# A latent-diffusion layer on one core: the second half of the second adaLN slab pair is multiplied as a high and a low part

## The chip, the core and the metric

The kernel runs on one core of one Trainium2 chip. The metric is the device time of one execution in microseconds; the median of three runs of the kernel before is 637.93 us (636.94 to 639.37). The numbers of the profile come from one further execution of the same program, recorded by the hardware profiler.

## The reference, cut to what matters

One layer of a latent-diffusion backbone works on 1024 latent tokens of width 1024, with one conditioning vector `c`, 256 context tokens and one learned vector `c_ctx`.

```python
def adaln(cond, w_ada, b_ada):
    m = jax.nn.silu(cond) @ w_ada + b_ada
    return jnp.split(m, 3, axis=-1)          # shift, scale, gate

shift, scale, gate = adaln(c, w_ada, b_ada)
shift_c, scale_c, gate_c = adaln(c_ctx, w_ada, b_ada)
h  = rmsnorm(x, norm_g) * (1 + scale[:, None]) + shift[:, None]
hc = rmsnorm(ctx, norm_g) * (1 + scale_c) + shift_c
q, k, v, za, u, bg, cg, zc = jnp.split(h @ w_in, SPLIT_POINTS, axis=-1)
...
attn = neighbourhood_attention(...) * silu(za)
conv = bg * conv3(cg * u) * silu(zc)
out  = x + gate[:, None] * (concat([attn, conv]) @ w_out)
```

The change is in the first line of `adaln`: the product of the two silu vectors (for `c` and for `c_ctx`, two columns side by side) with the shift and scale columns of `w_ada`.

## The kernel before, in words

**Number formats.** Nearly all matrix products are made as three products of two-part numbers: an operand is split into a high part, rounded to the reduced fp32 format (`F32R`), and a low part, which is the rest. ScalarE makes the high part (`act.copy`, shown as CAST), VectorE the low part (`dve.tensor_tensor(..., ALU.subtract)`).

**Stages.** In the first stage (up to about 78 us of the profile) the kernel loads x, the adaLN columns of `w_ada` and the first weight columns of `w_in`. It makes the modulation vectors `ab` (shift and scale by feature, for `c` and for `c_ctx`), the normed, transposed and modulated activations `h` (eight tiles `hh[k]`, `hl[k]`, high and low, one for each 128 features), and with each finished `h[k]` three columns of projections (`first_columns`, accumulators `acc`). Then come 32 projection tiles (`pacc`), 32 attention steps with further projections between them (`pu`), and the output projection (`pout`).

**The adaLN slabs.** The 2 x 1024 columns (shift, scale) are taken in four groups m = 0..3 of 256 shift columns (j = 0) and 256 scale columns (j = 1). `load_slab(m, j)` loads 1024 rows of 256 columns as `slabs[m, j]`, 128 partitions by 8 by 256. `products(m, j)` multiplies the slab, eight contraction steps, into one PSUM tile `mods[m]`, columns 0 to 255 for j = 0 and 256 to 511 for j = 1. For m = 0 and 1 this is done in fp32 with `c2`, the two silu columns. For m = 2 and 3 `split(m, j, part)` first makes `highs[j]` and `lows[j]` (names `slabh` and `slabl` in the profile), in two halves of four contraction steps, and `products` multiplies both with `c4`, four columns: the two silu columns in high part and their low part. The result then has four rows. `row_copy(m)` copies these to SBUF, `modulation(m)` transposes them and adds them up into the columns `ab[:, 2m:2m+2]`, with two further additions on VectorE if there are four rows. Group m is needed for `turn(half, 2m)` and `turn(half, 2m+1)`: `turn` writes the modulated high part with ScalarE (`h<-tr,ab`), the fp32 value with ScalarE or VectorE (`hw<-tr,ab`), and the low part with VectorE (`h<-hw,h`). `half` is 0 for the first 512 tokens and 1 for the other 512.

**Order.** In the first stage all engines and the SyncE queue run strictly in the order in which the code is written (`strict[:] = every + [sp]`): each instruction is chained behind the one before it on its engine. Loads come from SyncE in the order slabs (0,0) and (0,1), x tiles 0 to 3, weight chunk 0, x 4 and 5, chunk 1, x 6 and 7, slabs (1,0) and (1,1), chunks 2 and 3, slab (2,0). Slabs (1,·), (2,·) and (3,·) share three buffers, so that slab (2,1) waits for the buffer of (1,0), and slab (3,0) for that of (1,1). The stretch around the change, lines 769 to 802, is in the profile from 18 to 40 us.

**Places in SBUF.** The small constants, `c2`, `c4` and `ab` among them, lie in a pool `cp`, and nearly all tiles that are allocated on that side of SBUF lie behind it: x tiles (`xx`), weight chunks (`wr`, `wh`, `wl`), most attention tiles, and half of the output weights. The slabs and the activations `h` are allocated from the other side.

Of the kernel before, what the change touches and what calls it, by code (L numbers as in the profile page):

```python
# [10 lines left out]
F32 = mybir.dt.float32  # L11
# [8 lines left out]
P = 128  # L20
# [3 lines left out]
KT = D // P  # L24
# [15 lines left out]
def body(tc, es, x, ctxt, w_ada, b_ada, w_in, q_g, k_g, rpbr, w_out, vecs, cst, out):  # L40
# [21 lines left out]
    pe, act, dve, pool = every = [ordered(e) for e in (nc.tensor, nc.scalar, nc.vector, nc.gpsimd)]  # L62
    sp = ordered(nc.sync)

    def sbuf(name, side=None, bufs=1):
        kw = {} if side is None else {"side": side}
        return tc.tile_pool(name=name, bufs=bufs, reuse_waits="tile", **kw)
# [43 lines left out]
    cp = es.enter_context(sbuf("cp"))  # L111
# [17 lines left out]
    c2 = cp.tile([P, KT, 2], F32, name="c2")  # L129
# [10 lines left out]
    def place(k, shape, dtype, name):  # L140

        return hpool.tile(shape, dtype, name=name, tag=f"h{k}")
# [385 lines left out]
    def tr():  # L528
        return ps0.tile([P, 512], F32, name="tr", tag="tr", bufs=2)

    strict[:] = every + [sp]
    xx, slabs, highs, lows, chunks, mods, pts = {}, {}, {}, {}, {}, {}, {}
# [6 lines left out]
    def load_slab(m, j):  # L539

        new = place(6 + j, [P, KT, 256], F32, "slab") if m == 0 else sl.tile([P, KT, 256], F32, name="slab", tag="slab", bufs=3)
        n = 2 if m == 0 else 1
        for i in range(n):
            rows = slice(KT // n * i, KT // n * (i + 1))
            sp.dma_start(new[:, rows], bass.AP(w_ada.tensor, w_ada.offset + j * D + 256 * m + 3 * D * P * rows.start,
                                               [[3 * D, P], [3 * D * P, KT // n], [1, 256]]))
        slabs[m, j] = new

    def load_chunks(ks):
        for k in ks:  # L550
            chunks[k] = chunk_load(CU, k)
# [20 lines left out]
    def keep_clock(n):  # L572

        for _ in range(n):
            pe.matmul(acc0[2][1], warm[:, :P], warm, start=True, stop=True)
# [6 lines left out]
    dve.tensor_scalar(b1, bsc, 1.0, None, ALU.add)  # L582
    c4 = cp.tile([P, KT, 4], F32R, name="c4")
    act.copy(c4[:, :, 0:2], c2)
    keep_clock(7)
    dve.tensor_tensor(c4[:, :, 2:4], c2, c4[:, :, 0:2].bitcast(F32), ALU.subtract)

# [12 lines left out]
    def norm(xtile, n):  # L600
        dve.tensor_scalar(xtile, xtile, sums[n], None, ALU.mult)

    def split(m, j, part):

        if part == 0:
            highs[j] = hcp.tile([P, KT, 256], F32R, name="slabh", tag="AB"[j])
            lows[j] = place(6 + j, [P, KT, 256], F32R, "slabl")
        rows = slice(4 * part, 4 * part + 4)
        act.copy(highs[j][:, rows], slabs[m, j][:, rows])
        dve.tensor_tensor(lows[j][:, rows], slabs[m, j][:, rows], highs[j][:, rows].bitcast(F32), ALU.subtract)  # L610

    def products(m, j, kts=range(KT)):

        if m not in mods:
            mods[m] = tr()
        rows = mods[m][:2 if m < 2 else 4, 256 * j:256 * j + 256]
        parts = [(c2, slabs[m, j])] if m < 2 else [(c4, highs[j]), (c4, lows[j])]
        for i, (c, part) in enumerate(parts):
            for kt in kts:
                pe.matmul(rows, c[:, kt], part[:, kt], start=(i == 0 and kt == 0 and j == 0),  # L620
                          stop=(i == len(parts) - 1 and kt == KT - 1 and j == 1), skip_group_check=True)

    def row_copy(m):
        n = 2 if m < 2 else 4
        rw = cvp.tile([4, 512], F32, name="rw", tag="ub", bufs=2)
        (act.copy if m else dve.tensor_copy)(rw[:n], mods[m][:n])
        return rw[:n]

    def modulation(m, rw):

        n, ks = 2 if m < 2 else 4, slice(2 * m, 2 * m + 2)
        pm = mods[m]
        for j in range(2):
            for i in range(2):
                pe.transpose(pm[:, n * (2 * j + i):n * (2 * j + i + 1)], rw[:, 256 * j + i * P:256 * j + (i + 1) * P],
                             ident[:n, :n])
        both = lambda v: v[:, ks].rearrange("p (k o) -> p k o", o=1).broadcast_to([P, 2, 2])
        abk = ab[:, ks].rearrange("p k (w j) -> p j k w", w=2)
        pm = pm[:, 0:4 * n].rearrange("p (j k w) -> p j k w", j=2, k=2)
        dve.tensor_tensor(abk[:, 0], pm[:, 0, :, 0:2], both(bsh), ALU.add)  # L640
        dve.tensor_tensor(abk[:, 1], pm[:, 1, :, 0:2], both(b1), ALU.add)
        if n > 2:
            for j in range(2):
                dve.tensor_tensor(abk[:, j], abk[:, j], pm[:, j, :, 2:4], ALU.add)
        dve.tensor_tensor(abk[:, 1], abk[:, 1], both(ng), ALU.mult)
# [22 lines left out]
    def transposed(half, k, ts=range(4)):  # L668
        if (half, k) not in pts:
            pts[half, k] = tr()  # L670
        for i in ts:
            pe.transpose(pts[half, k][:, i * P:(i + 1) * P], xx[4 * half + i][:, k * P:(k + 1) * P], ident)
# [20 lines left out]
    def first_columns(half, k, part=range(3)):  # L693

        wh, wl = chunks[k]
        h_, l_ = (v.rearrange("p (b r c) -> p b (r c)", b=8, r=16)[:, :, 64 * half:64 * half + 64]
                  for v in (hh[k], hl[k]))
        for i in part:
            for u in (0, 2, 1):
                uc = slice(u * P, (u + 1) * P)  # L700
                pe.matmul(acc0[u][half], (wl if i == 1 else wh)[:, uc], l_ if i == 2 else h_,
                          start=k == 0 and i == 0, stop=k == KT - 1 and i == 2)
# [38 lines left out]
    more_h(range(6))  # L741

    products(0, 0)
    products(0, 1)
    square(xx[0], 0)
    root(0)
    keep_clock(2)
    rw = row_copy(0)
    square(xx[1], 1)
    root(1)  # L750
    norm(xx[0], 0)
    square(xx[2], 2)
    root(2)
    modulation(0, rw)
    keep_clock(2)
    for t in range(1, 4):
# [18 lines left out]
        norm(xx[t - 1], t - 1)  # L775
    first_columns(0, 1)
    norm(xx[7], 7)
    products(1, 0)
    transposed(1, 0)
    turn(1, 0, act)  # L780
    load_slab(2, 1)
    load_chunks([4, 5])
    products(1, 1, range(0, 4))
    transposed(1, 1)
    products(1, 1, range(4, KT))
    load_slab(3, 0)
    split_chunk(2)
    turn(1, 1, act)
    first_columns(1, 0)
    rw = row_copy(1)  # L790
    split_chunk(3)
    split(2, 0, 0)
    load_slab(3, 1)
    load_chunks([6, 7])
    transposed(0, 2)
    modulation(1, rw)
    turn(0, 2, dve)
    split(2, 0, 1)
# [5 lines left out]
    for m in range(1, 4):  # L804
# [31 lines left out]
        if new:  # L836
            split_chunk(k + 2)
            products(m + 1, 1)
            rw = row_copy(m + 1)
# [4 lines left out]
        if new:  # L844
            modulation(m + 1, rw)
# [213 lines left out]
    def both(v, n, pair):  # L1059

        w = 256 if n % 4 == 0 else 384
        return v[:, pair[0][0]:pair[-1][0] + 1, :w]
# [122 lines left out]
    for n in range(NT + 3):  # L1185
# [53 lines left out]
        if 1 < n <= NT + 1:  # L1239
            m, r = n - 2, (n - 2) % NB  # L1240
# [228 lines left out]
```

## Time and profile before

| | |
|---|---|
| median of three runs | 637.93 us (636.94 to 639.37) |
| profiled execution | 636.79 us, of which 635.0 us is the span from the first to the last instruction |
| TensorE busy | 626.1 us, 99% of the span |
| VectorE, ScalarE, GpSimd busy | 436.5, 324.1, 130.4 us |
| TensorE granted clock | 0.999 of full speed |
| HBM | 88.09 MB read, 38.62 MB written |

A timeline row gives the start in us from the beginning of the span, the length in us from the first start to the last end in the row, the engine, the line of code, the operation, `out<-in`, the shape of the operand (partitions by elements), how many instructions the row merges, and in brackets the idle time of the engine ahead of it with what ended it. Nearly every line reads L55 because the engines are wrapped in a recorder, so tiles are told apart by name: `tr` is the PSUM tile used for transposes and for `mods`, `slab` the raw adaLN columns, `slabh` and `slabl` their two parts, `c` any of `c2`, `c4` (and `c0` in the kernel after). An fp32 product of one contraction step shows as two MATMUL records, one in the reduced format as one. MATMUL ends are modelled and run over the next start, so a stretch of TensorE is read from start to start.

### The profile page before, as it was taken

Reading aid. Unit: us, or ns where it says so; the run is one execution under the profiler, and the core shown is the slowest. Engines: PE = TensorE matmul, PEld = TensorE weight load, DVE = VectorE, ACT = ScalarE, POOL = GpSimd, SP = SyncE. Lnnn points to the kernel's source line nnn. Section 1 sums busy time; section 2 is a strip of 40 time slices with the busy share of each in tenths; the row PEclk is TensorE's granted clock in tenths of the full one; section 3 lists DMA queues with packets and bytes.
Section 4 is the critical chain, followed back from the end, with each engine's and each line's share of the span. In section 5 each row is a group of like instructions: output and inputs, shape, how many; then the busy total and the mean of one; then the engine's idle time right before and its main releaser. Section 6 shows DMA issues by size and latency. Waiting matters only on the chain.

```text
span 635.0 us, 10038 instructions
## 1 busy us (share of the span) xinstructions
PE 626.1 (99%) x3479; PEld 537.1 (85%) x3480; DVE 436.5 (69%) x819; ACT 324.1 (51%) x699; POOL 130.4 (21%) x140
## 2 busy tenths in 40 slices
PE   8999999999999999999999999999999999999997
PEld 3477899999899999888888888888888788888885
DVE  1677858765766845468898889988998964575111
ACT  3676835424624545345576658567775854451000
POOL 1305014123123222101122111111111112005221
PEclk9999999999999999999999999999999999999999
DMA  8972638866784994875383635683742233966421
GB/s 320 386 260 96 186 107 258 262 198 216 245 262 138 305 334 152 304 244 168 127 260 116 240 109 204 193 276 101 252 145 74 61 106 120 328 208 233 165 101 50
DMA packets 102863, 125.61 MB, mean 198 GB/s; under 512 B 9649, under 2 KB 71305, under 8 KB 101532
## 3 DMA queue, kind: packets, MB, share of 16 engines
q1 hardware_dynamic: 96348, 113.38, 53.9%
q10 hardware_dynamic: 6208, 11.05, 5.6%
q0 software_dynamic: 256, 0.54, 0.3%
q8 instruction: 27, 0.44, 0.3%
q14 instruction: 24, 0.20, 0.1%
HBM read 88.09 MB, written 38.62 MB: 200 GB/s over the span
## 4 chain that ended last, share of the span: by engine, by line
PE 91%; DVE 6%; ACT 1%; issue 1%; POOL 0%; DVEq 0%; ACTq 0%; POOLq 0%
PE pu L55 25%; PE pacc L55 21%; PE po L55 7%; PE acc L55 7%; PE tr L55 5%; PE pout L75 5%; PE pout L74 5%; PE pout L76 5%; PE cacc L55 4%; PE pss L55 3%; PE pmx L55 2%; DVE mx L55 2%; PE pc L55 2%; DVE sb L55 2%; PE trA L55 1%
## 5 line engine op out<-in xcount | busy, mean ns | idle before, releaser
L55 PE MATMUL pu<-h,uh 128*128 128x512 f32 x544 | 169.0, 392 | 0.0
L55 PE MATMUL pacc<-wh,h 128*128 128x384 f32 x512 | 135.1, 338 | 0.0
L55 PEld LDWEIGHTS pu<-h,uh 128*128 128x128 f32 x544 | 98.1, 188 | 16.9
L55 PE MATMUL pu<-h,ul 128*128 128x512 f32 x272 | 106.3, 391 | 0.0
L55 PEld LDWEIGHTS pacc<-wh,h 128*128 128x128 f32 x512 | 92.8, 188 | 0.1
L55 POOL TENSOR_TENSOR plc<-sc,phc 128x512 fp32r<-128x512 f32 x32 | 43.0, 1345 | 215.5 <-ACT sc L55 159.0
L55 PE MATMUL pacc<-wl,h 128*128 128x384 f32 x256 | 85.6, 334 | 0.0
L55 POOL TENSOR_TENSOR ss<-ss,few 128x4 f32<-128x4 f32 (+1 forms) x40 | 41.4, 1037 | 126.3 <-DVE ss L55 126.1
L55 DVE TENSOR_TENSOR mx<-mx,sb 128x384 f32<-128x384 f32 (+1 forms) x64 | 59.4, 936 | 2.0
L55 PEld LDWEIGHTS pu<-h,ul 128*128 128x128 f32 x272 | 51.1, 188 | 11.3
L75 PE MATMUL pout<-wol,yh 128*128 128x512 f32 x128 | 49.8, 389 | 0.0
L76 PE MATMUL pout<-woh,yl 128*128 128x512 f32 x128 | 49.5, 389 | 0.0
L74 PE MATMUL pout<-woh,yh 128*128 128x512 f32 x128 | 48.3, 389 | 0.0
L55 PEld LDWEIGHTS pacc<-wl,h 128*128 128x128 f32 x256 | 48.1, 188 | 0.1
L55 DVE TENSOR_REDUCE ss<-sq 128x4 f32<-128x260 f32 (+1 forms) x40 | 15.8, 394 | 42.4 <-ACT sq L55 42.4
L55 ACT ACTIVATE sq<-pacc 128x256 f32<-128x256 f32 x32 | 12.3, 384 | 54.4 <-PE pacc L55 53.9
L1401 DVE TENSOR_TENSOR ot<-pout,gate 128x512 f32<-128x512 f32 x16 | 10.8, 689 | 40.5 <-PE pout L76 37.7
L55 ACT COPY mg<-pmx 128x256 f32<-128x256 f32 x32 | 11.9, 372 | 51.9 <-PE pmx L55 45.3
L1402 POOL TENSOR_TENSOR ot<-ot,xr 128x512 f32<-128x512 f32 x15 | 20.0, 1345 | 68.2 <-DVE ot L1401 67.0
L55 ACT COPY sc<-pc 128x512 f32<-128x512 f32 x32 | 18.8, 588 | 25.5 <-PE pc L55 25.5
L55 ACT ACTIVATE qn<-pacc,ss 128x64 f32<-128x64 f32 x128 | 30.0, 329 | 3.0 <-issue 2.5
L55 DVE TENSOR_TENSOR pll<-sb,phl 128x768 fp32r<-128x768 f32 (+2 forms) x33 | 28.4, 861 | 4.5 <-ACT sb L55 4.5
(155 smaller groups left out, 1280.9 us busy)
## 6 DMA issues: line engine op xcount, KB each, us to landing
uraw<-in_w_in SPq DMA_DIRECT2D x34, 256.0 KB
q_d<-qs SPq DMA_DIRECT2D x32, 256.0 KB
k_s<-k_d SPq DMA_DIRECT2D x8, 1024.0 KB
q_s<-q_d SPq DMA_DIRECT2D x16, 512.0 KB
wr<-in_w_in SPq DMA_DIRECT2D x40, 192.0 KB
slab<-in_w_ada SPq DMA_DIRECT2D x6, 1024.0 KB
v_d<-vs SPq DMA_DIRECT2D x20, 260.0 KB
v<-v_d SPq DMA_DIRECT2D x16, 325.0 KB
```

What stands on the lines that cost most here:

```text
L55: i = emit(*a, **kw)
L74: i = pe.matmul(ps, ah, bh, start=first, stop=False)
L75: pe.matmul(ps, ah, bl, start=False, stop=False)
L76: pe.matmul(ps, al, bh, start=False, stop=last)
L1401: dve.tensor_tensor(ot, ps, gate[:, cols], ALU.mult)
L1402: (dve if (nh, t) == (1, NB - 1) else pool).tensor_tensor(ot, ot, xr, ALU.add)
```

## The change

The scale half of the second group, (1,1), is multiplied like groups 2 and 3: `split(1, 1, 0)` and `split(1, 1, 1)` make its high and low part on ScalarE and VectorE, and `products(1, 1)` multiplies both with `c4`. Both halves of a group write the same four-row result, so the shift half (1,0), still multiplied in fp32, takes a new `c0`: the two silu columns and two columns of zeros. Group 1 now has four rows in `row_copy` and `modulation`. In `products` the new argument `parts` says which of the high (0) and low (1) part a call multiplies.

```diff
     c4 = cp.tile([P, KT, 4], F32R, name="c4")
     act.copy(c4[:, :, 0:2], c2)
+    c0 = cp.tile([P, KT, 4], F32, name="c0")
+    pool.memset(c0[:, :, 2:4], 0.0)
+    act.copy(c0[:, :, 0:2], c2)
...
-    def products(m, j, kts=range(KT)):
+    def products(m, j, kts=range(KT), parts=(0, 1)):
...
-        rows = mods[m][:2 if m < 2 else 4, 256 * j:256 * j + 256]
-        parts = [(c2, slabs[m, j])] if m < 2 else [(c4, highs[j]), (c4, lows[j])]
-        for i, (c, part) in enumerate(parts):
-            for kt in kts:
+        rows = mods[m][:4 if m else 2, 256 * j:256 * j + 256]
+        split_ = [(c4, highs[j]), (c4, lows[j])] if (m, j) >= (1, 1) else [(c0 if m else c2, slabs[m, j])]
+        for i, (c, part) in enumerate(split_):
+            for kt in kts if i in parts else ():
...
-        n = 2 if m < 2 else 4
+        n = 4 if m else 2
...
     norm(xx[7], 7)
+    split(1, 1, 0)
+    split(1, 1, 1)
     products(1, 0)
     transposed(1, 0)
     turn(1, 0, act)
     load_slab(2, 1)
     load_chunks([4, 5])
-    products(1, 1, range(0, 4))
+    products(1, 1, parts=(0,))
+    products(1, 1, range(4), (1,))
     transposed(1, 1)
-    products(1, 1, range(4, KT))
+    products(1, 1, range(4, KT), (1,))
     load_slab(3, 0)
     split_chunk(2)
     turn(1, 1, act)
```

TensorE, from the end of the first `first_columns` block on. `tr<-slab` is the fp32 product, `tr<-ci,xx` the transposes of `transposed(1, 0)` and `transposed(1, 1)`, `acc<-h` the start of `first_columns(1, 0)`. Before:

```order
80 L55 MATMUL tr<-slab,c_123 2x256 x8
81 L55 MATMUL tr<-ci,xx 128x128 x4
82 L55 MATMUL tr<-slab,c_123 2x256 x4
83 L55 MATMUL tr<-ci,xx 128x128 x4
84 L55 MATMUL tr<-slab,c_123 2x256 x4
85 L55 MATMUL acc_192<-h_219,wh 128x512
```

After:

```order
80 L55 MATMUL tr<-slab,c_211 4x256 x8
81 L55 MATMUL tr<-ci,xx 128x128 x4
82 L55 MATMUL tr<-slabh,c_209 4x256 x8
83 L55 MATMUL tr<-slabl,c_209 4x256 x4
84 L55 MATMUL tr<-ci,xx 128x128 x4
85 L55 MATMUL tr<-slabl,c_209 4x256 x4
86 L55 MATMUL acc_192<-h_222,wh 128x512
```

Eight fp32 steps of the second half became eight steps on the high and eight on the low part; nothing else stands elsewhere on this engine.

ScalarE, from the last squares of x to the row copy. `h<-tr,ab` and `hw<-tr,ab` are the two activations of `turn(1, 0)` and `turn(1, 1)`, `wh<-wr` the high part of weight chunk 2. Before:

```order
10 L55 ACTIVATE sqj,xss<-xx 128x1024 x3
11 L55 ACTIVATE h_219<-tr,ab 128x8x8x8
12 L55 ACTIVATE hw<-tr,ab 128x512
13 L55 CAST wh<-wr 128x384
14 L55 ACTIVATE h_220<-tr,ab 128x8x8x8
15 L55 ACTIVATE hw<-tr,ab 128x512
16 L55 COPY rw<-tr 2x512
```

After:

```order
11 L55 ACTIVATE sqj,xss<-xx 128x1024 x3
12 L55 CAST slabh<-slab 128x1024 x2
13 L55 ACTIVATE h_222<-tr,ab 128x8x8x8
14 L55 ACTIVATE hw<-tr,ab 128x512
15 L55 CAST wh<-wr 128x384
16 L55 ACTIVATE h_223<-tr,ab 128x8x8x8
17 L55 ACTIVATE hw<-tr,ab 128x512
18 L55 COPY rw<-tr 4x512
```

Two casts of 128 by 1024 now stand ahead of `turn(1, 0)`. VectorE likewise has the two subtractions `slabl<-slab,slabh` between the last x tile's norm and `turn(1, 0)`, and two further additions in `modulation(1)`.

More of the change, by code (lines that the diff above doesn't have):

```diff
@@ L610, in split @@
         dve.tensor_tensor(lows[j][:, rows], slabs[m, j][:, rows], highs[j][:, rows].bitcast(F32), ALU.subtract)
-    def products(m, j, kts=range(KT)):
+    def products(m, j, kts=range(KT), parts=(0, 1)):
         if m not in mods:
             mods[m] = tr()
-        rows = mods[m][:2 if m < 2 else 4, 256 * j:256 * j + 256]
-        parts = [(c2, slabs[m, j])] if m < 2 else [(c4, highs[j]), (c4, lows[j])]
-        for i, (c, part) in enumerate(parts):
-            for kt in kts:
+        rows = mods[m][:4 if m else 2, 256 * j:256 * j + 256]
+        split_ = [(c4, highs[j]), (c4, lows[j])] if (m, j) >= (1, 1) else [(c0 if m else c2, slabs[m, j])]
+        for i, (c, part) in enumerate(split_):
+            for kt in kts if i in parts else ():
                 pe.matmul(rows, c[:, kt], part[:, kt], start=(i == 0 and kt == 0 and j == 0),
-                          stop=(i == len(parts) - 1 and kt == KT - 1 and j == 1), skip_group_check=True)
+                          stop=(i == len(split_) - 1 and kt == KT - 1 and j == 1), skip_group_check=True)
     def row_copy(m):
-        n = 2 if m < 2 else 4
+        n = 4 if m else 2
         rw = cvp.tile([4, 512], F32, name="rw", tag="ub", bufs=2)
@@ L629, in modulation @@
     def modulation(m, rw):
-        n, ks = 2 if m < 2 else 4, slice(2 * m, 2 * m + 2)
+        n, ks = 4 if m else 2, slice(2 * m, 2 * m + 2)
         pm = mods[m]
```

## The prediction

> **What bounds the kernel now.** I read the page's busy times and its chain first. TensorE is busy nearly all the time and the chain that ends last runs through it.
>
> ```profile
> PE 626.1 (99%) x3479; PEld 537.1 (85%) x3480; DVE 436.5 (69%) x819; ACT 324.1 (51%) x699; POOL 130.4 (21%) x140
> ...
> PE 91%; DVE 6%; ACT 1%; issue 1%; POOL 0%; DVEq 0%; ACTq 0%; POOLq 0%
> ```
>
> So a microsecond of TensorE work that goes should come off the end, if TensorE doesn't wait for something in its place. The list of waits of TensorE's matmuls is short. Apart from the start of the program the longest in the first stage is this one (total in us, how often, the longest):
>
> ```profile
> PE acc L55 <- ACT h L55: 0.8, 1, 0.8
> ```
>
> It stands ahead of the first block of `first_columns`, before the stretch of the change. From there on the first stage has no wait of TensorE at all: it is work laid end to end, and the other engines are just early enough. The timeline of TensorE around the change:
>
> ```profile
> 28.12 1.89 PE L55 MATMUL tr<-slab,c 128*2 128x256 f32 x8
> 29.94 0.66 PE L55 MATMUL tr<-ci,xx 128*128 128x128 f32 x4
> 30.53 1.89 PE L55 MATMUL tr<-slab,c 128*2 128x256 f32 x8
> 32.34 0.98 PE L55 MATMUL acc<-h,wh 128*128 128x512 f32 x3
> ...
> 37.95 0.95 PE L55 MATMUL acc<-h,wh 128*128 128x512 f32 x3
> ...
> 39.42 0.86 PE L55 MATMUL acc<-h,wh 128*128 128x512 f32 x3
> ...
> 40.48 1.17 PE L55 MATMUL tr<-slabh,c 128*4 128x256 f32 x8
> ...
> 42.39 0.86 PE L55 MATMUL acc<-h,wh 128*128 128x512 f32 x3
> ```
>
> The 28.12 and 30.53 rows are half (1,1), the half that changes, around the transposes of `transposed(1, 1)`. The stretch from 40.48 to 42.39 is half (2,0), high and low part, which is already done in the new way.
>
> **The change part by part: what goes from TensorE.** Half (1,1) takes 29.94 - 28.12 = 1.82 and 32.34 - 30.53 = 1.81, together 3.63 us. In the new way the same eight steps take 42.39 - 40.48 = 1.91 us. The difference is 1.72 us. Half (1,0) keeps its fp32 product with four columns in place of two. The bounds are nothing, since the 256 streamed elements stay the same, and a lengthening in the weight load; the rows of the tile `c` (minimum, median and maximum in ns) show the load of four columns at 84 ns beside 85 for two, so I take nothing.
>
> ```profile
> L55 PEld LDWEIGHTS tr<-slab,c x64: 80/85/85, 6.5 to 31.8; 128*2 128x2 f32 x64
> L55 PEld LDWEIGHTS tr<-slabh,c x32: 83/84/87, 40.4 to 59.5; 128*4 128x4 f32 x32
> ```
>
> **What is added early.** The copy into `c0` stands on ScalarE ahead of the first square of x, for which this engine waits 5.90 us anyway:
>
> ```profile
> 11.04 1.06 ACT L55 ACTIVATE sqj<-xx 128x1024 bf16<-128x1024 f32 x1 [5.90 <-DMA xx<-in_x]
> ```
>
> The copy is of 16 columns and costs nothing inside that wait; without the cover it would be less than the 1.06 us of the square. The memset on GpSimd is ahead of the first power, which follows that square, and has the same cover.
>
> **What is added to ScalarE and VectorE, and when slab (1,1) lands.** ScalarE gets two casts and VectorE two subtractions of 128 by 1024. Both stand ahead of `turn(1, 0)`. Everything behind them on these engines waits until the slab has landed. The trace shows no wait for it, so I bound the landing. No later than 28.12: TensorE reads it there without waiting. For the earlier side I follow the queue. ScalarE's square of x tile 4 was released by that tile's load at 16.68. Behind it come x 5, chunk 1, x 6, x 7, slabs (1,0) and (1,1). By their shapes (128x1024, 128x384, 128x2048 floats) that is 3 x 0.524 + 0.197 + 2 x 1.049 = 3.87 MB, and the transfers ran at 386 GB/s:
>
> ```profile
> 16.68 1.06 ACT L55 ACTIVATE sqj<-xx 128x1024 bf16<-128x1024 f32 x1 [0.25 <-DMA xx<-in_x]
> ```
>
> ```profile
> 16.68:26.68 10.00, 9.20 (x43) 5.23 (x42) 8.00 (x16) 6.35 (x11) 4.07 (x5) 1.00 1.07 386
> ```
>
> 3.87 / 0.386 = 10.0 us, so about 26.7. I take 26.7, and keep 26.3 to 28.1.
>
> **What then waits for what.** The rows of ScalarE and VectorE that carry the lengths:
>
> ```profile
> 28.23 0.78 ACT L55 ACTIVATE h<-tr,ab 128x512 fp32r<-128x512 f32 x1 [4.33 <-PE tr L55]
> 28.91 0.77 ACT L55 ACTIVATE hw<-tr,ab 128x512 f32<-128x512 f32 x1
> 29.57 0.50 ACT L55 CAST wh<-wr 128x384 fp32r<-128x384 f32 x1
> 30.64 0.78 ACT L55 ACTIVATE h<-tr,ab 128x512 fp32r<-128x512 f32 x1 [0.56 <-PE tr L55]
> 31.31 0.77 ACT L55 ACTIVATE hw<-tr,ab 128x512 f32<-128x512 f32 x1
> 32.45 0.57 ACT L55 COPY rw<-tr 2x512 f32<-2x512 f32 x1 [0.37 <-PE tr L55]
> 32.93 0.51 ACT L55 CAST wh<-wr 128x384 fp32r<-128x384 f32 x1
> 33.35 1.04 ACT L55 CAST slabh<-slab 128x1024 fp32r<-128x1024 f32 x1
> 36.08 0.78 ACT L55 ACTIVATE h<-tr,ab 128x512 fp32r<-128x512 f32 x1 [1.69 <-DVE ab L55]
> ```
>
> ```profile
> 34.42 1.22 DVE L55 TENSOR_TENSOR slabl<-slab,slabh 128x1024 fp32r<-128x1024 f32 x1 [0.39 <-ACT slabh L55]
> ...
> 37.74 0.69 DVE L55 TENSOR_TENSOR h<-hw,h 128x512 fp32r<-128x512 f32 x1
> ```
>
> ScalarE stood idle for 4.33 us ahead of 28.23: that is where the casts go. At 1.04 each they run from 26.7 to 28.8, and VectorE, at 1.22 each, follows from 27.8 to 30.2. TensorE comes to the high part at 28.12. Its first four steps need the first cast (27.7); its next four, half of half the 1.91 later at 28.6, the second (28.8): a wait of 0.2. The first low steps, at about 29.2, need the first subtraction (29.0); the last, after the transposes at 30.3, the second (30.2). So `first_columns(1, 0)` starts at about 30.8 in place of 32.34: 1.5 us gained.
>
> Behind the casts stands the rest. `turn(1, 0)` starts on ScalarE at 28.8 in place of 28.23, takes 29.57 - 28.23 = 1.34, and chunk 2's cast 0.50. So `turn(1, 1)` starts at 30.6, the row copy 1.34 later at 32.0, and the first cast of slab (2,0) 33.35 - 32.45 = 0.90 after that, at 32.9. Before, that was 33.35: this chain moves up by 0.5, TensorE by 1.5. From that cast to `turn(0, 2)` it is 36.08 - 33.35 = 2.73 through VectorE, which subtracts ahead of the modulation, and now 0.2 more for two additions (this row has such a pair):
>
> ```profile
> 48.28 0.23 DVE L55 TENSOR_TENSOR ab<-ab,tr 128x4 f32<-128x4 f32 x2
> ```
>
> So `turn(0, 2)` starts at 35.8 and its high part is there at 36.6; TensorE wants it for `first_columns(0, 2)` at 37.95 - 1.5 = 36.45. The low part starts 37.74 - 36.08 = 1.66 after, ends 0.69 later at 38.15, and is wanted at 39.42 - 1.5 = 37.9. TensorE waits about 0.2 us there, and behind that the rows show no step as close. Slab (3,0) takes the buffer of (1,1), which is free when VectorE has split it (30.2) and not only when TensorE has multiplied it (32.3): earlier, also for the queue on SyncE, whose order is unchanged.
>
> **The sum.** -1.72 + 0.2 + 0.2 = -1.3 us. The profiled execution of 636.79 us (span 635.0, and 1.8 around it) would become 635.5. It lies 1.1 below the median of the runs, and I take the difference from the median: 637.93 - 1.3 = 636.6 us, 0.2% faster. About 0.5%, 3.2 us, is what a measurement of this kernel can tell from no change, so this counts as no change.
>
> **The rivals.** *The chain takes it back.* ScalarE and VectorE become the bound between 26 and 40 us. If slab (1,1) lands only at the bound of 28.1, all that was worked out above for these two engines is 1.4 later, and `first_columns(0, 2)` gets its low part at 39.5, when it wanted it before (39.42). The gain is then 0 to 0.5: 637.4 to 637.9. The room of 0.1 to 0.2 us at most steps speaks for it, the 386 GB/s against it.
>
> *Slower: the place of the tiles.* `c0` takes 8 x 4 x 4 = 128 bytes in each partition of a pool ahead of nearly everything on that side of SBUF, and moves all of it by 128 bytes; in the built program most of those tiles started on a multiple of 256 bytes and no longer do. If the streamed weight tiles `wh` and `wl` were read more slowly from there, the price would be large, since `pacc` alone is busy for 135.1 + 85.6 = 220.7 us:
>
> ```profile
> L55 PE MATMUL pacc<-wh,h 128*128 128x384 f32 x512 | 135.1, 338 | 0.0
> ...
> L55 PE MATMUL pacc<-wl,h 128*128 128x384 f32 x256 | 85.6, 334 | 0.0
> ```
>
> From 2% longer on (4.5 us against the 1.3 gained) the kernel is slower by over 0.5%; at 3% it takes 636.6 + 6.6 = 643.2. Against it: the transposes load x tiles, which start on such a multiple, and tiles `rot`, which start 96 bytes past one, as weights in the same 140 ns. No row shows it for a streamed tile.
>
> ```profile
> L55 PEld LDWEIGHTS tr<-ci,xx x64: 138/140/143, 15.0 to 71.9; 128*128 128x128 f32 x64
> L55 PEld LDWEIGHTS trA<-ci,rot x32: 138/140/143, 104.2 to 269.3; 128*128 128x128 f32 x32
> ```
>
> *Loads to moved tiles slow down.* The x tiles and chunks lie behind `c0` too. Up to slab (1,1) they are 8 x 0.524 + 2 x 0.197 = 4.6 MB, 11.9 us at 386 GB/s. With 5% more, 0.6 us, the slab lands at 27.3 and TensorE waits 0.6 more: 637.2. No row shows a load slowed by its place. The Trainium skill, DMA: Bandwidth & Descriptors, How a descriptor splits into AXI transactions, speaks for this rival: a transfer that doesn't start on a multiple of 256 bytes begins at the boundary below and pays for the bytes between. By it a 512-byte chunk row would take 20 beats in place of 16 and a 4096-byte x row 132 in place of 128, an estimate of 0.6 us in all. No run here shows it yet.
>
> *Faster by over 0.5%.* It needs 3.2 us and the work that goes is 1.72. That leaves the scatter of the runs (the lowest of three is 1.0 below the median) and gains later that no row suggests.
>
> **How the numbers follow.** My forecast, 636.6, gets 0.57; the chain that takes it back, 637.7, 0.20; slower loads, 637.2, 0.05; the place of the tiles, 643.2, 0.09; faster than 634.7 for a reason that I don't see, 0.09. The first three lie within 0.5%; of my forecast I give 0.05 to the faster side and 0.01 to the slower, for scatter. So faster 0.14, same 0.76, slower 0.10. The range goes from 634.3, the whole 1.72 with the scatter of the low side (-1.0) and some of the faster case, to 639.4, no gain with the scatter of the high side (+1.4). It leaves out most of the slower case and part of the faster one.
>
> **What would show it.** Right: in the profile after, the stretch from 28.1 us to `first_columns(1, 0)` is about 2.7 us in place of 4.2, the first cast `slabh` starts near 26.7 after a wait for the slab's load, and TensorE waits a few tenths for `h` at `first_columns(0, 2)`; everything behind is 1.3 us earlier, with `pacc` at the same mean. The chain would show in casts near 28, or in waits of TensorE for `slabl` or `h` of over 1 us in sum; the place, in `pacc` with another mean; the loads, in squares of x that are released later than 11.04 and 16.68. I am wrong if TensorE's stretch shortens by 1.5 and the end doesn't move with it.

## The result and the profile after

The changed kernel takes 639.63 us (median of 19 runs, 638.63 to 640.43); the kernel before, run beside it, 637.71 us (19 runs, 636.49 to 639.37). The ratio is 1.0031, with an interval of 1.0024 to 1.0037: 1.9 us slower, where 1.3 us faster was forecast. That is above the upper end of the range, 639.4.

The page of the kernel after, its span and its busy times:

```profile
span 637.5 us, 10047 instructions
...
PE 627.4 (98%) x3479; PEld 539.0 (85%) x3480; DVE 439.0 (69%) x823; ACT 326.1 (51%) x702; POOL 130.4 (20%) x141
```

TensorE was to lose about 1.7 us of work. It is busy for 1.3 us more (627.4 beside 626.1). So what was lost isn't a new wait of the size of the loss; some of TensorE's work became longer. First the place of the change, TensorE's timeline after:

```profile
28.43 1.33 PE L55 MATMUL tr<-slabh,c 128*4 128x256 f32 x8
29.60 0.63 PE L55 MATMUL tr<-slabl,c 128*4 128x256 f32 x4
30.48 0.66 PE L55 MATMUL tr<-ci,xx 128*128 128x128 f32 x4 [0.25 <-ACT hw L55]
30.89 0.71 PE L55 MATMUL tr<-slabl,c 128*4 128x256 f32 x4
31.45 0.85 PE L55 MATMUL acc<-h,wh 128*128 128x512 f32 x3
...
37.16 0.97 PE L55 MATMUL acc<-h,wh 128*128 128x512 f32 x3
...
39.88 1.16 PE L55 MATMUL tr<-slabh,c 128*4 128x256 f32 x8
```

From half (1,1) to `first_columns(1, 0)` it is 31.45 - 28.43 = 3.02 us in place of 4.22. That is 1.20 us gained where 1.5 was forecast. One small wait, for `hw`, is in no step of the forecast.

Then the stages. The next two fences are TensorE's timelines of before and of after: the first block of `first_columns`, and the first instruction of the projections, of the attention steps and of the output projection.

```profile
19.47 0.96 PE L55 MATMUL acc<-h,wh 128*128 128x512 f32 x3 [0.76 <-ACT h L55]
...
77.86 0.34 PE L55 MATMUL pacc<-wh,h 128*128 128x384 f32 x1
...
269.68 0.48 PE L55 MATMUL pss<-q_s,k_s 128*128 128x256 f32 x2
...
543.33 0.84 PE L74 MATMUL pout<-woh,yh 128*128 128x512 f32 x3
```

```profile
19.93 0.96 PE L55 MATMUL acc<-h,wh 128*128 128x512 f32 x3 [0.76 <-ACT h L55]
...
77.60 0.34 PE L55 MATMUL pacc<-wh,h 128*128 128x384 f32 x1
...
270.89 0.48 PE L55 MATMUL pss<-q_s,k_s 128*128 128x256 f32 x2
...
544.63 0.85 PE L74 MATMUL pout<-woh,yh 128*128 128x512 f32 x3
```

| stage, from start to start | before | after | difference |
|---|---|---|---|
| `first_columns` and what follows, to the first `pacc` | 58.39 | 57.67 | -0.72 |
| projections, to the first `pss` | 191.82 | 193.29 | +1.47 |
| attention steps, to the first `pout` | 273.65 | 273.74 | +0.09 |
| output projection, to the end of the span | 91.7 | 92.9 | +1.2 |

The first block starts between 19.1 and 20.2 us in the profiles, among kernels that differ in nothing ahead of it too (f4, below, at 21.5), so lengths of stages are compared and not times from the start of the span. The stage that was changed got shorter by about half of what was forecast, and two stages in which no instruction changed got longer. The groups of the page after:

```profile
L55 PE MATMUL pacc<-wh,h 128*128 128x384 f32 x512 | 136.4, 341 | 0.0
...
L55 PE MATMUL pacc<-wl,h 128*128 128x384 f32 x256 | 86.4, 338 | 0.0
```

Before, these means were 338 and 334 ns. The output projection, grouped from 590 to 625 us, where it is in its second half of columns, before and after:

```profile
L74 PE MATMUL pout<-woh,yh 128*128 128x512 f32 x52 | 20.2, 389 | 0.0
```

```profile
L74 PE MATMUL pout<-woh,yh 128*128 128x512 f32 x51 | 20.1, 394 | 0.0
```

No wait stands ahead of either. Each of these matmuls is about 1% longer.

### The profile page after: what moved, and what is told of

Read it like the earlier page. It is cut to its first block, busy times and chain, and to the rows that moved or that the text cites. A ratio compares the mean times of both kernels' runs of the same rounds, so it can differ in the third digit from the quotient of the medians.

```text
span 637.5 us, 10047 instructions
## 1 busy us (share of the span) xinstructions
PE 627.4 (98%) x3479; PEld 539.0 (85%) x3480; DVE 439.0 (69%) x823; ACT 326.1 (51%) x702; POOL 130.4 (20%) x141
## 4 chain that ended last, share of the span: by engine, by line
PE 83%; DVE 7%; DMA 4%; ACT 3%; POOL 1%; issue 1%; SPq 1%; DVEq 0%; ACTq 0%
PE pu L55 25%; PE pacc L55 21%; PE po L55 7%; PE pout L74 5%; PE pout L76 5%; PE pout L75 5%; PE cacc L55 4%; PE pss L55 3%; PE acc L55 2%; PE pmx L55 2%; DVE mx L55 2%; PE pc L55 2%; DMA slab<-in_w_ada 2%; DVE sb L55 2%; DMA xx<-in_x 2%; PE tr L55 1%
## 5 line engine op out<-in xcount | busy, mean ns | idle before, releaser
L1408 POOL TENSOR_TENSOR ot<-ot,xr 128x512 f32<-128x512 f32 x15 | 20.2, 1353 | 69.0 <-DVE ot L1407 66.2
```

What stands on the lines that cost most here:

```text
L1408: (dve if (nh, t) == (1, NB - 1) else pool).tensor_tensor(ot, ot, xr, ALU.add)
```

## The experiments

The theory after the result was that the new products gain what was forecast, and that the 128 bytes of `c0`, which move all tiles behind it in SBUF, cost more than that. In the built program h, `uh`, the raw slabs and the output weights of the second half of columns (`woh1x`) are allocated from the other side and stay on multiples of 256 bytes, and so does `y7`; x, `wr`, `wh`, `wl`, `hc`, the attention's q and k, y 0 to 6 and the output weights of the first half (`woh0x`) go to 128 bytes past one. The rival: the split itself costs, through its extra work on ScalarE and VectorE or later loads. `fill_up(pool, n)` is a helper of the kernel that allocates an unused tile of n bytes in each partition.

**f1: the changed kernel, with the tiles put back.** 128 bytes more behind `c0`, so that all is moved by 256.

```diff
     act.copy(c0[:, :, 0:2], c2)
+    fill_up(cp, 128)
```

> The changed kernel with 128 unused bytes behind c0, so that all tiles behind it lie 256 bytes further than before in place of 128. Theory A (the 128 bytes cost what was lost: a matmul is slower when its streamed tile and its weight tile lie 128 bytes apart in a multiple of 256, and loads into moved tiles are slower): pacc back to a mean of 338 and 334 ns, pout to 389 in all tiles, the first square of x at 11.0 us, and the time 1.0 to 1.7 us below the kernel before, about 636.3. Theory B (the split itself, its casts and what waits behind them, costs it): as the changed kernel, 1.9 us above the kernel before, about 639.6.

Measured: 636.32 us (635.73 to 637.56), ratio to before 0.9985 (0.9977 to 0.9993). One unused tile takes about 2.9 us off the changed kernel (0.9985 in place of 1.0031) and makes it faster than the kernel before. The page of f1 shows `pacc` back, its timeline the stages:

```profile
L55 PE MATMUL pacc<-wh,h 128*128 128x384 f32 x512 | 135.2, 338 | 0.0
...
L55 PE MATMUL pacc<-wl,h 128*128 128x384 f32 x256 | 85.7, 335 | 0.0
```

```profile
20.00 0.96 PE L55 MATMUL acc<-h,wh 128*128 128x512 f32 x3 [0.76 <-ACT h L55]
...
24.52 3.62 PE L55 MATMUL tr<-slab,c 128*4 128x256 f32 x16
...
28.48 1.20 PE L55 MATMUL tr<-slabh,c 128*4 128x256 f32 x8
...
31.28 0.86 PE L55 MATMUL acc<-h,wh 128*128 128x512 f32 x3
...
36.98 0.96 PE L55 MATMUL acc<-h,wh 128*128 128x512 f32 x3
...
39.71 1.16 PE L55 MATMUL tr<-slabh,c 128*4 128x256 f32 x8
...
77.08 0.34 PE L55 MATMUL pacc<-wh,h 128*128 128x384 f32 x1
...
268.92 0.48 PE L55 MATMUL pss<-q_s,k_s 128*128 128x256 f32 x2
```

The first stage takes 77.08 - 20.00 = 57.08 us, 1.31 less than before; the projections take 191.84, as before.

**f2 and f3: the kernel before, with nothing but the move.** `fill_up(cp, 128)` and `fill_up(cp, 256)` behind the copy into `c4`.

```diff
     act.copy(c4[:, :, 0:2], c2)
+    fill_up(cp, 128)
```

> The kernel before with 128 unused bytes where c0 stands, and no other change. Theory A: pacc at 341 and 338 ns, pout of the second half of the columns at 394, the first square of x 0.3 to 0.5 us later; 1.5 + 1.2 + 0.4 = 3.1 us slower than the kernel before, about 640.8. Theory B: no change, 637.7.

> The kernel before with 256 unused bytes at that place. Theory A, with 256 bytes as the period: no change, 637.7, and the matmuls' means as before. If any move of the tiles costs (theory A without a period): as with 128 bytes, 640.8. Theory B: no change.

Measured: f2 640.33 us (640.21 to 640.49), ratio 1.0046 (1.0033 to 1.0058); f3 637.17 us, ratio 0.9997 (0.9988 to 1.0006). Without any of the change's instructions, 128 bytes cost 2.9 us and 256 bytes nothing. The projections of f2 take 272.16 - 78.87 = 193.29 us like those of the kernel after, those of f3 191.84. That is the loss, without the change. The timeline and the group of f2:

```profile
78.87 0.34 PE L55 MATMUL pacc<-wh,h 128*128 128x384 f32 x1
...
272.16 0.48 PE L55 MATMUL pss<-q_s,k_s 128*128 128x256 f32 x2
```

```profile
L55 PE MATMUL pacc<-wh,h 128*128 128x384 f32 x512 | 136.5, 341 | 0.0
```

**f4: both sides of SBUF moved.** f2, and 128 bytes in the pool of the other side too, so that h, `uh`, the slabs and the rest of the output weights move as well.

```diff
+    vp = es.enter_context(sbuf("vp", side="right"))
+    vecT = vp.tile([P, nvec], F32, name="vecT")
...
+    fill_up(vp, 128)
...
+    fill_up(cp, 128)
```

> The kernel before with 128 unused bytes on both sides of SBUF, so that all tiles, h and the second half of the output weights too, are off a multiple of 256 by 128, and streamed and weight tiles differ by a multiple of 256 again. If the distance between streamed and weight tile decides: pacc back at 338 and 334 ns, pout at 389, and only slower loads are left, 0.3 to 0.9 us, about 638.3. If the place of the streamed tile alone decides: pacc at 341 and 338, pout at 394, and pu slower too, 641 or more.

Measured: 638.64 us (637.85 to 640.53), ratio 1.0017 (1.0008 to 1.0026). The page of f4:

```profile
L55 PE MATMUL pacc<-wh,h 128*128 128x384 f32 x512 | 135.2, 338 | 0.0
```

Every tile of these matmuls lies off a multiple of 256 bytes, and they take 338 ns as before; the projections take 191.83 us, and `pout` is back at 389 ns in its second half. For these two it isn't the place of a tile that counts but the place of the streamed tile and of the weight tile relative to each other. The total stayed about 1 us above before. The profiled execution is the slowest of f4's twelve (640.53 us), so it doesn't show for certain what the others pay; in it the first stage took 59.17 us in place of 58.39, and the first half of the output projection waited, which the groups from 545 to 580 us show:

```profile
L74 PE MATMUL pout<-woh,yh 128*128 128x512 f32 x49 | 17.7, 391 | 0.5 <-ACT yh L1382 0.5
```

**f7 and f8: one pair at a time.** f7 moves what the output projection's pool holds (y 0 to 6 and `woh0x`), f8 only `wh` and `wl`, with a second tile of 128 bytes behind them so that x stays.

```diff
     op = es.enter_context(sbuf("op"))
+    fill_up(op, 128)
```

```diff
+        if not padded:
+            fill_up(wpp, 128)
         wh = wpp.tile([P, 384], F32R, name="wh", tag="wh", bufs=12)
         wl = wpp.tile([P, 384], F32R, name="wl", tag="wl", bufs=12)
+        if not padded:
+            wpp.tile([P, 32], F32, name="pad2")
+            padded.append(1)
```

> The kernel before with 128 unused bytes at the start of the pool of the output stage: the first half of the output weights and seven of the eight pairs of y tiles move, the second half of the weights and the eighth pair don't. If the distance between the streamed and the weight tile decides: pout of the second half of the columns 5 ns slower per matmul, of the first half only at the eighth pair; 1.2 us in all, about 638.3. If it is the place of the streamed tile: the first half slower, the second not.

> The kernel before with 128 unused bytes ahead of the split weight chunks wh and wl and 128 behind them, so that these two alone are off by 128. If the distance decides: pacc at 341 and 338 ns, 1.5 us, about 638.6; cacc slower too, since its weights hc don't move this time; loads and pout as before. Otherwise no change.

Measured: f7 638.71 us (637.82 to 640.98), ratio 1.0019 (1.001 to 1.0028); f8 638.63 us (637.93 to 639.48), ratio 1.0018 (1.0009 to 1.0026). Each is about 1.2 us slower than before. The page of f7, and its output projection from 590 to 625 us:

```profile
L55 PE MATMUL pacc<-wh,h 128*128 128x384 f32 x512 | 135.2, 338 | 0.0
```

```profile
L74 PE MATMUL pout<-woh,yh 128*128 128x512 f32 x51 | 20.1, 394 | 0.0
```

The groups of f8:

```profile
L55 PE MATMUL pacc<-wh,h 128*128 128x384 f32 x512 | 136.3, 341 | 0.0
...
L55 PE MATMUL cacc<-wh,hc 128*128 128x256 f32 x128 | 23.4, 281 | 0.0
```

f7 lengthens `pout` alone, and f8 mainly `pacc` (the projections take 193.05 us; its first stage, where `acc` has `wh` and `wl` as weights, is 0.2 longer too). The output projection even shows the pairs within one kernel: y 0 to 6 and `woh0x` are both moved in the first half and it is at 390 ns there (y7, which stays, makes up one pair in eight); against `woh1x`, which wasn't moved, it is at 394. That 394 is a mean. From start to start the matmuls of the second half take between 226 and 241 ns in f7, and before all of them 226 or 227, and which of an output tile's 24 are the slow ones is nearly the same in f2, f7 and the kernel after. So the distance modulo 256 isn't all that sets the cost; what else does is open. `cacc`, which has the moved `wh` as its weight tile and streams 256 columns of `hc`, got shorter by 2 ns (281; before, f1 and f4 show 283), so the sign isn't the same for every matmul.

**f6 and f10: another distance.** f6 moves everything behind `c4` by 64 bytes; f10 is f1 with `wh` and `wl` alone 64 bytes past a multiple of 256.

```diff
+        if not padded:
+            fill_up(wpp, 64)
         wh = wpp.tile([P, 384], F32R, name="wh", tag="wh", bufs=12)
         wl = wpp.tile([P, 384], F32R, name="wl", tag="wl", bufs=12)
+        if not padded:
+            wpp.tile([P, 48], F32, name="pad2")
+            padded.append(1)
```

> The kernel before with 64 unused bytes where c0 stands. If each distance that is not a multiple of 256 costs the same: as with 128 bytes, pacc at 341 and 338 ns, pout of the second half at 394, 3.1 us above the kernel before. If the cost grows with the distance: about half, 339.5 and 336, 1.5 us. If 64 is harmless for the matmuls: only the loads, 0.5 us.

> The changed kernel with everything behind c0 back on multiples of 256 bytes, and wh and wl alone at 64 bytes past one. By the theory that any distance of streamed and weight tile that isn't a multiple of 256 costs, pacc is over 338 and 334 ns and its stage about 192.5 us or more, and the time 637 to 638. By the theory that 64 bytes cost pacc nothing (as the stage read with all tiles moved by 64 suggests), the stage is 191.4 to 191.9 us and the time 635.9 to 636.5, as with the fill alone.

Measured: f6 638.92 us (638.23 to 641.53), ratio 1.0022 (1.0012 to 1.0033): the second half of `pout` is at 394 ns, as with 128 bytes, but the projections take 191.38 us, less than before. f10 is 635.88 us (635.03 to 636.6), ratio 0.9973 (0.9962 to 0.9984), the fastest of all. Its timeline and groups:

```profile
77.00 0.34 PE L55 MATMUL pacc<-wh,h 128*128 128x384 f32 x1
...
267.90 0.48 PE L55 MATMUL pss<-q_s,k_s 128*128 128x256 f32 x2
```

```profile
L55 PE MATMUL pacc<-wh,h 128*128 128x384 f32 x512 | 135.3, 339 | 0.0
...
L55 PE MATMUL cacc<-wh,hc 128*128 128x256 f32 x128 | 23.3, 280 | 0.0
```

The projection stage is 267.90 - 77.00 = 190.90 us long, 0.9 below f1 and below what either theory expected. The mean of one `pacc` rose to 339 ns all the same: the ends are modelled, and a start-to-start time is what counts. Summed from start to start, the 768 matmuls of `pacc` give 0.4 us of the 0.9 and the 192 of `cacc` another 0.4. So a distance of 64 bytes costs the 512-column matmuls of `pout` as much as 128 does, and the 384-column ones of `pacc` nothing. Why is open, and so is what makes `cacc` shorter in f8 and f10.

**f5 and f9: the loads.** f5 moves the x tiles alone by 128 bytes, f9 the raw chunks `wr` alone.

```diff
     xp = xs.enter_context(sbuf("xp"))
+    fill_up(xp, 128)
```

```diff
     wpp = wps.enter_context(sbuf("wpp"))
+    fill_up(wpp, 128)
...
+        if not padded:
+            wpp.tile([P, 32], F32, name="pad2")
+            padded.append(1)
         wh = wpp.tile([P, 384], F32R, name="wh", tag="wh", bufs=12)
```

> The kernel before with 128 unused bytes at the start of the pool of the x tiles alone; this pool closes with the first stage, and nothing else moves. If loads into moved tiles are slower: from the release of the first square of x to that of the fifth 5.9 us in place of 5.64, and the end 0.3 to 0.6 us later, about 637.5; pacc and pout as before. If the loads were not slower but only scattered: 5.64 and no change.

> The kernel before, with only the raw weight chunks wr moved to 128 bytes past a multiple of 256; wh, wl and the x tiles stay on multiples. No matmul reads wr, so by the theory that the place of streamed tile and weight tile relative to each other sets TensorE's time, pacc and pout keep 338, 334 and 389 ns and the time is 636.9 to 637.9 us. By the theory that the 512-byte rows of the chunks are what loads more slowly to a moved place, the squares of x tile 0 and x tile 4 are released 5.7 to 5.8 us apart in place of 5.64, since chunk 0 lies between them, and the same from x 4 to x 7; by the theory that it needs both the x tiles and the chunks moved, 5.64 to 5.70.

Measured: f5 637.33 us, ratio 0.999 (0.9979 to 1.0001); f9 637.53 us, ratio 1.0 (0.9992 to 1.0009). What loads cost is read from the squares of x tile 0 and x tile 4 on ScalarE, both released by their loads. In the kernel after, in f5 and in f9:

```profile
11.49 1.06 ACT L55 ACTIVATE sqj<-xx 128x1024 bf16<-128x1024 f32 x1 [6.24 <-DMA xx<-in_x]
...
17.39 1.06 ACT L55 ACTIVATE sqj<-xx 128x1024 bf16<-128x1024 f32 x1 [0.38 <-DMA xx<-in_x]
```

```profile
11.27 1.06 ACT L55 ACTIVATE sqj<-xx 128x1024 bf16<-128x1024 f32 x1 [6.12 <-DMA xx<-in_x]
...
16.96 1.06 ACT L55 ACTIVATE sqj<-xx 128x1024 bf16<-128x1024 f32 x1 [0.25 <-DMA xx<-in_x]
```

```profile
11.42 1.06 ACT L55 ACTIVATE sqj<-xx 128x1024 bf16<-128x1024 f32 x1 [6.26 <-DMA xx<-in_x]
...
17.14 1.06 ACT L55 ACTIVATE sqj<-xx 128x1024 bf16<-128x1024 f32 x1 [0.35 <-DMA xx<-in_x]
```

Before it is 5.64 us from the one to the other; in f1 and f3, with all tiles on multiples of 256 bytes, 5.68 and 5.64. After it is 5.90 (f2 5.87, f6 5.89), with x alone moved 5.69, with the chunks alone 5.72. Loads to moved tiles are slower, then, by about 0.26 us in these 5.6. Each part alone adds 0.05 to 0.08, and f7, which moves neither, shows 5.69 too, so in this stretch neither part can be told from scatter, and the two don't add up to the whole; why is open.

Later in the first stage the chunks alone can be read. Near 65 us ScalarE casts four of them one after the other. Before, and in f9:

```profile
65.53 2.23 ACT L55 CAST wh<-wr 128x384 fp32r<-128x384 f32 x4 [0.43 <-DMA wr<-in_w_in]
```

```profile
66.18 0.51 ACT L55 CAST wh<-wr 128x384 fp32r<-128x384 f32 x1 [0.53 <-DMA wr<-in_w_in]
66.87 0.51 ACT L55 CAST wh<-wr 128x384 fp32r<-128x384 f32 x1 [0.17 <-DMA wr<-in_w_in]
67.54 0.52 ACT L55 CAST wh<-wr 128x384 fp32r<-128x384 f32 x1 [0.16 <-DMA wr<-in_w_in]
68.21 0.51 ACT L55 CAST wh<-wr 128x384 fp32r<-128x384 f32 x1 [0.16 <-DMA wr<-in_w_in]
```

In f9 each waits for its load and they start 0.68 us apart; before it is (2.23 - 0.51) / 3 = 0.57. The kernel after, f2, f4 and f6 have 0.68 as well, f5 and all kernels with `wr` in place 0.57. So a moved chunk lands more slowly by about a fifth, with no other tile moved. What it costs TensorE is small: ScalarE comes later to its next work, and TensorE waits for that at the transposes of `xc`, 0.28 us in f9, and in the kernel after as this row shows:

```profile
69.05 0.66 PE L55 MATMUL tr<-ci,xc 128*128 128x128 f32 x4 [0.19 <-ACT hw L55]
```

The first stage of f9 is 58.64 us in place of 58.39; its median doesn't show that.

## Why the prediction was wrong

**What goes from TensorE, and the waits: right, by f1.** The forecast was -1.3 us; f1's first stage is 1.31 shorter and its median 0.8 below its own before (by the ratio 1.0, interval 0.4 to 1.5). Step by step, with the rows of f1 against those of before, where half (1,0) begins with this row:

```profile
23.99 3.62 PE L55 MATMUL tr<-slab,c 128*2 128x256 f32 x16
```

From its start to `first_columns(1, 0)` it is 31.28 - 24.52 = 6.76 in place of 32.34 - 23.99 = 8.35, so 1.59 gained where 1.5 was forecast; to `first_columns(0, 2)` 5.70 in place of 5.61; from there to slab (2,0) 2.73 in place of 2.53. The last two take 0.29 back, where 0.2 was forecast. The two misses of 0.09 cancel, so that the sum fits to 0.01 is luck.

**The landing of slab (1,1): right.** The first cast waits for that load in the kernel after as well:

```profile
27.09 1.99 ACT L55 CAST slabh<-slab 128x1024 fp32r<-128x1024 f32 x2 [2.73 <-DMA slab<-in_w_ada]
```

It starts 27.09 - 17.39 = 9.70 us after the square of x tile 4, forecast 10.0.

**One wait was overlooked, and small.** `transposed(1, 1)` waits 0.25 us for `hw`: the `tr` tile has two buffers, one of which holds the products of the group, and ScalarE must have read the transposes of (1,0) out of the other before the next can be written. The forecast delayed `turn(1, 0)` on ScalarE by 0.6 us and didn't ask who needs its tile back. In f1 this wait is 0.14 us, and the one of 0.2 that was forecast at the second cast isn't there (the eight high steps go from 28.48 to 29.52), so it doesn't show in the sum. In the kernel after both are there: the fifth high step starts 0.27 us after the fourth, at 29.14, where its neighbours are 0.12 apart, and the second cast ended at 29.08.

**Loads to moved tiles: the rival was real, and its 0.6 us came about, though not where it put them.** It slowed the loads by 0.26 us up to x tile 4, and in the kernel after the stretch of TensorE is 3.02 us where f1 has 31.28 - 28.48 = 2.80. So 0.2 of the 0.6 that the rival expected at slab (1,1) came there; how the rest of the first stage's 0.6 came is said below, and that the sizes agree is partly luck. The Trainium skill, DMA: Bandwidth & Descriptors, How a descriptor splits into AXI transactions, would give, as an estimate by its beats, 0.3 us for the same four x tiles and one chunk (4 x 0.524 MB x 4/128 + 0.197 MB x 4/16 = 0.115 MB, at 386 GB/s). With both moved the trace agrees; with x alone (0.05 in place of 0.17) or the chunk alone (0.08 in place of 0.13) it shows less than that rule, while the four chunks of f9 near 65 us show 0.11 each (0.68 - 0.57), close to its 0.13. The section speaks of the bytes that are fetched, and here it is the destination that moved, so the rule is carried over and no run shows its beats.

**The step that failed: the rival "the place of the tiles".** The forecast's sum, -1.72 + 0.2 + 0.2, has no term for the 128 bytes that `c0` takes; what they do to matmuls stood in it at nothing. The runs show 1.47 us in the projections and 1.2 us in the output projection in its place. The mechanism was named, with `pacc` and the streamed `wh`, and then given 9 in 100. Three things in its working were wrong. Its evidence against, weights loaded from two places in the same 140 ns, is about a weight load alone, while f4 shows that it is the pair of streamed and weight tile that counts. Its point of decision, 2% of `pacc` alone, was set for a loss of over 0.5%, though a third of a percent is a loss that nineteen runs tell from nothing; what `pacc` needed to eat the gain was 1.3 of 220.7 us, 0.6%, and it got 1.47 us. And it looked at `pacc` only: `pout` lies in moved tiles too, and took 1.2 us. The sum that the runs give is -1.3 (products) + 0.6 (first stage, after against f1) + 1.45 (projections) + 0.1 (attention) + 1.2 (output projection) = +2.05, measured +1.9. Of the 0.6, 0.22 is the stretch at the slab above. About 0.2 more is lost around the transposes of `xc`: from the transposes ahead of them it is 69.05 - 68.26 = 0.79 us in place of 68.36 - 67.92 = 0.44 in f1, and part of it is won back behind them. The rest goes in steps too small to place; f8, where no load moved, lost 0.2 in this stage as well.

## What to carry to other kernels

A small tile added at the head of a pool moves every tile behind it, and in a kernel that TensorE bounds this can cost more than the edit gains. Look at the addresses before and after, and fill up to what was there. When a change is slower than its own arithmetic, run the old kernel with nothing but the side effect (here one unused tile), and the new one without it; the two runs f1 and f2 settled the cause. A rival that touches hundreds of microseconds of matmuls needs only half a percent to win, so price it by the gain that it has to eat and not by what would be large.

## What the runs showed of the hardware

- The time of a matmul in this kernel depends on the addresses of its streamed tile and of the weight tiles relative to each other. At a distance of 128 bytes modulo 256 the 384-column ones of `pacc` have a mean of 341 ns in place of 338, and the stage with 768 of them is 1.47 us longer; the 512-column ones of `pout` 394 in place of 389. At 256 bytes (f3), or with both moved by 128 (f4), there is no difference. The distance modulo 256 isn't the whole of it: at 128 bytes single matmuls of `pout` take 226 to 241 ns from start to start in f7, where before all take 226 or 227.
- It isn't one-sided: at 64 bytes those of 512 columns are as slow as at 128, those of 384 are not slower from start to start, and those of 256 columns have a mean of 280 ns in place of 283, at 128 bytes 281.
- Loads to tiles 128 or 64 bytes off a multiple of 256 are slower where x and weight chunks are both off (5.64 to 5.90 us up to x tile 4). Four chunks in a row, moved alone by 128 bytes, follow each other by 0.68 us in place of 0.57; moved x tiles alone show no difference clear of scatter (5.69, and 5.69 in a kernel that moves neither).
